# Weight copies of the second projection one tile at a time and earlier, early weights of the first feed-forward layer split ahead, three square sums added by transfers

## The chip, the cores and the metric

The kernel runs on one core of a Trainium2 chip. The metric is device time in microseconds (us). Three runs of the kernel before took 1983.63, 1984.63 and 1985.36 us, with a median of 1984.63. The execution that the profiler recorded took 1982.42 us, and its trace spans 1980.6 us from the first instruction to the last.

TensorE (PE) does the matmuls, VectorE (DVE), ScalarE (ACT) and GpSimd (POOL) the element work. Transfers are issued by SyncE (SP) and by POOL and are carried out by 16 DMA engines that the two queues share.

## The reference, cut to what matters

Two layers on a sequence of 1024 tokens of width 1024, in float32. Each layer is a token mixer and then a SwiGLU channel mixer, each with an RMSNorm ahead and a residual sum behind:

```python
def reference(x, conv_w_in, conv_w, conv_w_out, attn_w_qkv, ...):
    for i in range(DEPTH):                       # DEPTH = 2
        h = rmsnorm(x, norm_mixer[i])
        if i % N_MIXERS == 0:                    # layer 0
            mix = short_conv_mixer(h, conv_w_in[j], conv_w[j], conv_w_out[j])
        else:                                    # layer 1
            mix = swa_sink_attention(h, ...)
        x = x + mix
        h = rmsnorm(x, norm_ffn[i])
        x = x + swiglu_ffn(h, ffn_w_gate_up[i], ffn_w_down[i])

def short_conv_mixer(h, w_in, conv_w, w_out):
    b_gate, c_gate, xv = jnp.split(h @ w_in, 3, axis=-1)
    u = b_gate * xv
    y = <causal convolution of u, 3 taps for each channel>
    return (c_gate * y) @ w_out

def swiglu_ffn(h, w_gate_up, w_down):
    g, u = jnp.split(h @ w_gate_up, 2, axis=-1)
    return (jax.nn.silu(g) * u) @ w_down
```

The change lies in layer 0: the product with `w_out` (the second projection of the convolution mixer), the RMSNorm behind it, and the first product of the channel mixer (`w_gate_up`, called `w_gu` in the kernel).

## The kernel before, in words

**Layout.** Activations are kept transposed: features on the 128 partitions, 1024 tokens along the free dimension, so the eight tiles X0 to X7 hold the whole residual. A token half (512 columns) is called `h` = 0 or 1.

**Three matmuls for one.** Weights and activations are each split into a rounded part (`hi`, a CAST on ACT, L925) and the rest (`lo`, a subtraction on DVE, L926), in a type that the PE multiplies fast. Three matmuls (hi by hi, hi by lo, lo by hi; lines L992, L993, L995) replace one float32 product.

**Seven products for eight.** The large products are done as a fast 2-by-2 block multiplication: seven products, numbered `k` = 0 to 6, of sums and differences of the weight quarters and of the activation quarters. A *granule* is one such product for one pair of output tiles `u`: 4 weight tiles of 128 x 128, 12 matmuls of 128 x 512. Three of the seven take a weight quarter as it is; the other four take a sum of quarters.

**Where the sums of weights come from.** For most units DVE makes them. For the first four units of a product the four sums are made in DRAM ahead of time: `added_sums` (L883) has SP copy the four quarters into a scratch tensor (`s`), L886, and then POOL issue four transfers that add one quarter onto another, L889. It is called for `w_out` (L383, scratch `s_389`, in two pairs of tiles u = 0 and 2) and, through `first_added_sums` (L896), for `w_gu` (scratch `s_0_112`). Each copy moves two tile pairs at once: 512 KB, rows of 2 KB.

**What sets the order.** An object `Line` holds a planned clock in us, in which a matmul counts 0.2265. `at(t, f)` puts a piece of work at a planned time, `work` puts matmuls at the end of the line. The pieces are then written out in the order of planned time, and every engine, SP and POOL among them, works through its own list in that order. So whatever waits on an engine holds up all that stands behind it there. In this kernel planned time 0 is 41.48 us in the trace.

**The ring of weights.** `ring_granule` (L999) gives each granule a load (L969, 256 KB, into one of two buffers named WR or one of two named WH) planned 20 us ahead of its matmuls (`LEAD + 7`, LEAD = 13) and a split (L925, L926, into one of eight G buffers) planned 13 us ahead. Units from the fifth on load 512 KB at a time, into the same WR and WH buffers (L629, L633).

**The first mixer's middle and end.** After the first projection's start (to 52 us in the trace) come its granules, first k = 0, 1, 6, 5, 2, 3, 4 for four units, then unit by unit. Products that go to the PSUM banks P0 and P1 use them in turn, so a bank has to be read out before the next but one granule begins; the `acc` banks are four. `lead_in` (L727) then does the second projection: while the last unit of the first is finished, sums of activation quarters are made by transfers that add (L731, POOL); the granules of `w_out` follow, k = 0 first, each with four units. Results of some go to X by ACT (L776) and get the residual by a transfer that adds `xT` (L777, POOL); others are added by DVE (L781).

**The norm behind it.** `tail_done` (L1138) runs when a half tile is finished: ACT squares it (L1146 the first time, into the sum `s0` or `s1`; L1149 afterwards, into G10 or G11), POOL stores it (L1152), and DVE adds the square to the sum (L1154). `half_chain` (L1159) has PE sum over the partitions (L1167), once per half, turn the result into rows (L1179), and `scale` (L1189) multiplies. The half 1 sum is needed while PE works on the first granules of the channel mixer.

Of the kernel before, what the change touches and what calls it, by code (L numbers as in the profile page):

```python
# [13 lines left out]
ALU = mybir.AluOpType  # L14

P = 128
# [56 lines left out]
GROUP = 4  # L73
HALF = T // 2
# [5 lines left out]
LEAD = 13.0  # L80
# [3 lines left out]
def trunk_kernel(ctx: ExitStack, tc: tile.TileContext, xT, small, w_in, w_out, w_qk, w_v, w_o, w_gu, w_dn, out):  # L84
# [212 lines left out]
    def conv_layer():  # L297
# [81 lines left out]
        out_sums = tc.dram_tile((4, GROUP, P, 5 * P), F32, name="s3")  # L379
        for u in (0, 2):  # L380
            dst = [out_sums[i, u : u + 2][:, :, 0 : 4 * P] for i in range(4)]
            parts = [w_out[2 * u + r : 2 * u + 4 : 2][:, :, c] for r in (0, 1) for c in (0, 1)]
            added_sums(dst, parts, line, 60.0 + 9.0 * u, 18.0)  # L383
        first_added_sums(0, line, 120.0, 18.0)
        at(-7.6, mean)
        at(-5.0, turn)
        tools = scheme(line, ["G0", "G3", "G6", "G7", "G1", "G2", "G4", "G5"])
# [329 lines left out]
        def out_product(u, k):  # L717
            srcs = {0: w_out[2 * u][:, 0], 1: w_out[2 * u][:, 1], 4: w_out[2 * u + 1][:, 1]}
            src = srcs[k] if k in srcs else out_sums[SUMS[k], u][:, 0 : 4 * P]
            name = {1: "d1", 5: "e", 6: "e"}.get(k, "d")  # L720
            tag = "acc" if k in (0, 2, 3, 4) else f"P{u % 2}" if k == 1 or u < 2 else "acc"
            get = bank_at(("out", u), name, tag)
            ring_granule(4, lambda: Z[k], 0, get, k in (0, 1, 5), True, src=src)
            odd, h = C_OF[k]
            return get, 2 * u + odd, h

        def lead_in(done):  # L727
            s = line.end

            def add_by_dma(to, of):  # L730
                nc.gpsimd.dma_start(to(), of(), accum_op=ALU.add)  # L731

            def add_here(out_, a, b):
                dve.tensor_tensor(out_(), a(), b(), ALU.add)

            def x_of(m, h):
                return xT[m * P : (m + 1) * P, halves[h]]

            def load_half(m, h):
                nc.sync.dma_start(Y[m][:, halves[h]], x_of(m, h))  # L740

            for j in range(NK):
                at(s + 5.0, lambda j=j: X.__setitem__(j, Y[j]))
            for p in range(4):
                b11, b12, b21, b22 = (lambda j=2 * p + odd, h=h: Y[j][:, halves[h]] for odd in (0, 1) for h in (0, 1))
                t2 = lambda p=p: z2(p)
                k0, k1, k2, k3, k4, k5, k6 = (
                    (-7.6, 0.3, 7.0, 11.0, 27.4, 4.6, 36.0),
                    (-6.5, 1.0, 9.8, 12.4, 28.5, 5.7, 37.1),
                    (-5.4, 2.4, 15.0, 13.8, 29.6, 8.6, 38.2),  # L750
                    (1.7, 17.3, 24.9, 25.9, 30.7, 24.0, 39.3),
                )[p]
                if p < 3:
                    t_1, t_c, t_2, t_3, t_4 = ((-4.4, 0.2, 1.6, 3.6, 8.2), (-3.5, 1.2, 2.6, 4.5, 9.2), (-2.6, 7.6, 9.4, 5.4, 15.0))[p]
                    at(s + t_1, add_by_dma, b11, b12)
# [12 lines left out]
                put_z(2, p, t2, s + k2)  # L768
                put_z(3, p, b12, s + k3, minus=True)
                put_z(4, p, b21, s + k4, minus=True)  # L770
                put_z(6, p, b22, s + k6)
                at(s + k4 + 3.5, load_half, 2 * p + 1, 0)

            def copy_out(get, m, h, t, sign):
                c = halves[h]
                at(t, lambda: act.activation(X[m][:, c], get(), AF.Copy, scale=sign))  # L776
                at(t + 0.9, lambda: nc.gpsimd.dma_start(X[m][:, c], x_of(m, h), accum_op=ALU.add))  # L777

            def add_out(get, m, h, t, op):
                c = halves[h]  # L780
                at(t, lambda: dve.tensor_tensor(X[m][:, c], X[m][:, c], get(), op))  # L781

            v = n_units - 1
            first = {}
            for k in (2, 5, 3):
                steady(v, k)
            for u in (0, 1):
                first[u] = out_product(u, 0)
            steady(v, 4)
            first[2] = out_product(2, 0)  # L790
            steady(v, 6)
            first[3] = out_product(3, 0)
            for k in range(1, KINDS):
# [12 lines left out]
            return begin1, line.end  # L806

        channel_mixer(
            0,
            2,  # L810
            None,
            [],
            raw_tags=None,
            extra_tags=None,
            keep_tags=None,
            line=line,
            lead_in=lead_in,
# [65 lines left out]
    def added_sums(dst, parts, line, t, gap):  # L883

        def copy(i):
            nc.sync.dma_start(dst[i], parts[i])  # L886
# [48 lines left out]
    def scheme(line, ring_tags, before=None):  # L935
# [60 lines left out]

                line.work(3, three)

        def ring_granule(n, ops_of, j, bank_of, start, stop, src=None, raw_of=None, room=None, split=True, lo_eng=dve):  # L999

            it = {}
            t = line.end
            if src is not None:
                at(t - LEAD - 7.0, load_raw, it, src, n)
                raw_of = lambda: it["raw"]
            if split:
                split_granule(it, raw_of, n, room or ring_room, t - LEAD, lo_eng)
# [46 lines left out]
    def channel_mixer(layer, next_stage, src_of, operands, raw_tags, extra_tags, keep_tags, slots, begin_with=(), first_w=None, line=None, lead_in=None, before=None):  # L1054
# [83 lines left out]
        def tail_done(h, m, t):  # L1138
            c = slice(h * HALF, h * HALF + HALF)
            first = h not in begun  # L1140
            begun.add(h)

            def square():
                if first:
                    state["ss", h] = slot(f"s{h}", (P, HALF))
                    act.activation(state["ss", h], X[m][:, c], AF.Square)  # L1146
                else:
                    units["sq", h, m] = slot(f"G{10 + m % 2}", (P, HALF))
                    act.activation(units["sq", h, m], X[m][:, c], AF.Square)  # L1149

            at(t + 0.8, square)
            at(t + 0.9, lambda: nc.gpsimd.dma_start(xres[m][:, c], X[m][:, c]))  # L1152
            if not first:
                at(t + 1.6, lambda: dve.tensor_tensor(state["ss", h], state["ss", h], units["sq", h, m], ALU.add))  # L1154


# [33 lines left out]

        whole = layer == 0
        if whole:
            begin1, begin2 = lead_in(tail_done)
        else:
            origin = line.end
            begin1 = origin + 8 * tail
            begin2 = origin + 16 * tail
            for h in (0, 1):
                for m in range(NK):
                    tail_item(h, m)  # L1200
# [18 lines left out]
                nc.sync.dma_start(pairs[0]["s2"][:, u], first_sums[layer][SUMS[2], u][:, 0 : 4 * P])  # L1219


        if not whole:
# [69 lines left out]
        def unit_product(u, k, tag, direct):  # L1292
# [3 lines left out]
            ops_of = lambda: B[k]  # L1296
            if u < GROUP:
                srcs = {0: w_gu[layer, u][:, 0], 1: w_gu[layer, u][:, 1], 4: w_gu[layer, NF + u][:, 1]}
                if k < 3 and not whole:
                    it = early[k, u]  # L1300
                    granule_work(it, 4, ops_of, 0, get, start, True)
                    if k < 2:
# [929 lines left out]
```

## Time and profile before

| | us |
|---|---|
| runs, median of 3 | 1984.63 |
| profiled execution, its own time | 1982.42 |
| its span | 1980.6 |
| PE busy in the span | 1929.6 |
| DVE busy in the span | 1285.6 |
| ACT busy in the span | 876.7 |
| POOL busy in the span | 272.9 |

How to read it: PE has work nearly all the time, so what matters are the places where it had none, and what it waited for there. A group line gives engine, line, operation, the tile written, the tiles read, busy time and mean duration. A wait line gives who waited, on what engine and line, the sum in us, how often, and the longest. A line of a window gives, for a stretch of time, the busy us of each engine with the number of instructions, then the TensorE clock that was granted (1.00 is full), the mean busy share of the 16 DMA engines, and the GB/s moved. Numbers such as L886 are lines of the kernel before; in the changed kernel the same code lies 4 to 17 lines further down.

### The profile page before, as it was taken

The page shows a single profiled execution, that of the slowest core. Times are in us where ns is not written, and L with a number is a line of the kernel's source. Part 1 is how long each engine was busy: PE and PEld are TensorE (multiplying, and loading weights), DVE is VectorE, ACT ScalarE, POOL GpSimd, SP SyncE. Part 2 cuts the span into 40 slices and gives each one's busy share as a digit, 9 for nine tenths or more (in the row PEclk, how much of TensorE's full clock was granted, in tenths as well). Part 3 has the DMA queues.
Part 4 walks back from the last instruction along what each step waited for, and adds up shares of the span by engine and source line. Part 5 has one row for each costly group of instructions (what it writes and reads, how often), then busy time and mean ns, then how long its engine had stood idle before and what let it go on. Part 6 is the DMA issues. An engine that isn't in the chain of part 4 may idle for free.

```text
span 1980.6 us, 25183 instructions
## 1 busy us (share of the span) xinstructions
PE 1929.6 (97%) x9105; PEld 1612.1 (81%) x9105; DVE 1285.6 (65%) x2222; ACT 876.7 (44%) x1741; POOL 272.9 (14%) x370
## 2 busy tenths in 40 slices
PE   9976998999999999999999999999999999999999
PEld 8854887788888888888888888888888888888887
DVE  8964875876665656556644777788666566575543
ACT  5522354453333334344523888755333333344442
POOL 0000023101111110010012446410010111110000
PEclk9997999999999999999999999999999999999999
DMA  8433889455665663996420000051565665467562
GB/s 317 161 108 104 241 171 220 145 181 164 207 190 152 189 171 137 360 290 208 162 75 12 22 17 17 27 181 59 207 190 170 193 182 172 130 235 272 202 223 104
DMA packets 131404, 325.35 MB, mean 164 GB/s; under 512 B 13392, under 2 KB 24784, under 8 KB 131280
## 3 DMA queue, kind: packets, MB, share of 16 engines
q1 hardware_dynamic: 101280, 228.81, 33.2%
q0 software_dynamic: 29856, 94.91, 19.5%
q8 instruction: 71, 1.16, 0.2%
q14 instruction: 53, 0.43, 0.1%
q10 hardware_dynamic: 144, 0.03, 0.0%
HBM read 261.31 MB, written 130.55 MB: 198 GB/s over the span
## 4 chain that ended last, share of the span: by engine, by line
PE 85%; DVE 5%; DMA 5%; issue 3%; ACT 1%; POOL 1%; POOLq 0%; ACTq 0%; DVEq 0%
PE acc L992 14%; PE acc L993 14%; PE acc L995 14%; PE P L992 8%; PE P L993 8%; PE P L995 8%; PE acc L167 6%; DMA WR<-in_w_in 4%; PE acc L171 3%; PE P L1857 1%; DVE G L926 1%; PE P L1681 1%; PE P L1882 1%; PE acc L1122 1%; PE acc L1124 1%
## 5 line engine op out<-in xcount | busy, mean ns | idle before, releaser
L992 PE MATMUL acc<-XS,G 128*128 128x512 f32 x942 | 368.5, 391 | 18.9 <-ACT G L555 18.9
L993 PE MATMUL acc<-XS,G 128*128 128x512 f32 x942 | 367.6, 390 | 0.0
L995 PE MATMUL acc<-XS,G 128*128 128x512 f32 x942 | 367.4, 390 | 0.0
L992 PE MATMUL P<-A,G 128*128 128x512 f32 x534 | 209.7, 393 | 21.2 <-DVE G L543 14.1
L992 PEld LDWEIGHTS acc<-XS,G 128*128 128x128 f32 x942 | 177.6, 189 | 56.2 <-ACT G L555 19.3
L993 PE MATMUL P<-A,G 128*128 128x512 f32 x534 | 208.8, 391 | 0.0
L995 PE MATMUL P<-A,G 128*128 128x512 f32 x534 | 208.7, 391 | 0.0
L995 PEld LDWEIGHTS acc<-XS,G 128*128 128x128 f32 x942 | 177.6, 189 | 37.2
L993 PEld LDWEIGHTS acc<-XS,G 128*128 128x128 f32 x942 | 177.7, 189 | 36.7
L926 DVE TENSOR_TENSOR G<-WR,G 128x512 fp32r<-128x512 f32 (+1 forms) x218 | 145.8, 669 | 70.0 <-ACT G L925 69.4
L925 ACT CAST G<-WR 128x512 fp32r<-128x512 f32 (+1 forms) x218 | 131.8, 605 | 111.5 <-DMA WR<-in_w_in 49.4
L992 PE MATMUL acc<-A,G 128*128 128x512 f32 x458 | 178.3, 389 | 0.0
L995 PE MATMUL acc<-A,G 128*128 128x512 f32 x458 | 178.2, 389 | 0.0
L993 PE MATMUL acc<-A,G 128*128 128x512 f32 x458 | 178.2, 389 | 0.0
L926 DVE TENSOR_TENSOR G<-WL,G 128x512 fp32r<-128x512 f32 x168 | 114.9, 685 | 69.5 <-ACT G L925 69.5
L167 PE MATMUL acc<-XS,WH 128*128 128x512 f32 x480 | 148.0, 408 | 0.5 <-ACT WH L139 0.4
L925 ACT CAST G<-WH 128x512 fp32r<-128x512 f32 (+1 forms) x176 | 105.9, 602 | 87.4 <-PE acc L995 43.2
L992 PEld LDWEIGHTS P<-A,G 128*128 128x128 f32 x534 | 101.0, 189 | 43.5 <-DVE G L543 15.0
L926 DVE TENSOR_TENSOR G<-WH,G 128x512 fp32r<-128x512 f32 (+1 forms) x176 | 116.9, 664 | 20.2 <-ACT G L925 20.1
L1290 ACT ACTIVATE G<-G 128x512 f32<-128x512 f32 x88 | 55.8, 634 | 160.4 <-DVE G L1361 156.3
L925 ACT CAST G<-WL 128x512 fp32r<-128x512 f32 x168 | 103.4, 615 | 37.8 <-DVE WL L878 21.3
L995 PEld LDWEIGHTS P<-A,G 128*128 128x128 f32 x534 | 100.9, 189 | 21.2
(317 smaller groups left out, 3616.2 us busy)
## 6 DMA issues: line engine op xcount, KB each, us to landing
G<-h SPq DMA_DIRECT2D x70, 512.0 KB, 3.8
s<-in_w_dn SPq DMA_DIRECT2D x32, 704.0 KB, 7.9
h<-X POOLq DMA_DIRECT2D x44, 512.0 KB, 5.5
s<-s POOLq DMA_DIRECT2D x32, 704.0 KB, 7.4
WR<-in_w_gu SPq DMA_DIRECT2D x36, 512.0 KB, 4.8
WH<-in_w_gu SPq DMA_DIRECT2D x36, 512.0 KB, 3.8
h<-X POOLq DMA_DIRECT2D x66, 256.0 KB, 2.9
WR<-s SPq DMA_DIRECT2D x62, 256.0 KB, 4.6
```

Source lines behind the costliest of these rows:

```text
L167: pe.matmul(ps.half(h), wh, xs[:, j, c], start=first and j == 0, stop=False)
L171: pe.matmul(ps.half(h), wl, xs[:, 0, c], start=False, stop=last)
L925: lambda: act.copy(out_hi, raw),
L926: lambda: lo_eng.tensor_tensor(out_lo, raw, plain(out_hi), ALU.subtract),
L992: pe.matmul(ps, w[:, 0, c], x[:, 0, :], start=start and e == 0, stop=False, skip_group_check=True)
L993: pe.matmul(ps, w[:, 0, c], x[:, 1, :], start=False, stop=False, skip_group_check=True)
L995: pe.matmul(ps, w[:, 1, c], x[:, 0, :], start=False, stop=last, skip_group_check=True)
L1122: pe.matmul(ps, hi[:, kc], xs[:, 0, c], start=k == 0, stop=False, skip_group_check=True)
L1124: pe.matmul(ps, lo[:, kc], xs[:, 0, c], start=False, stop=k == n_op - 1, skip_group_check=True)
L1290: state["silu"] = act.activation(x, x, AF.Silu)
L1681: pe.transpose(pb[:, t], wide[:, t], ident)
L1857: pe.transpose(ps[:, kb, e, :], s[:, e, kb * P : (kb + 1) * P], ident)
```

## The change

Five edits, all in layer 0:

1. The copies of `w_out` quarters are issued one tile pair at a time (16 copies of 256 KB, 128 rows each, where 8 copies of 512 KB took two tile pairs whose places in `w_out` are not adjacent), and planned from 30.0 on in steps of 4.5 us, the two groups 4 us apart; before from 60.0 on in steps of 9 us, the groups 18 us apart. The adding transfers follow at 9 us where they were 18 us apart.
2. The copies of `w_gu` quarters keep their shape (8 of 512 KB) and are planned from 74.0 on with half the spacing; before from 120.0.
3. The weights of the first four granules (k = 0) of the channel mixer are loaded into XS0 in four transfers and split into XS6 and XS7, planned 34.7 us behind the start `s` of `lead_in` and then every 2.72 us; before they went through the ring like the others.
4. The second projection's last granules (k = 6) are loaded and split 6 us earlier (`lead=19.0`).
5. For half 1, the squares of tiles 3, 5 and 7 are added to `s1` by transfers that POOL issues, not by DVE. The two buffers of the squares are used in turn (`m // 2`), where before all odd tiles shared one and all even tiles the other.

```diff
-            parts = [w_out[2 * u + r : 2 * u + 4 : 2][:, :, c] for r in (0, 1) for c in (0, 1)]
-            added_sums(dst, parts, line, 60.0 + 9.0 * u, 18.0)
-        first_added_sums(0, line, 120.0, 18.0)
+            parts = [[w_out[2 * (u + i) + r][:, c] for i in (0, 1)] for r in (0, 1) for c in (0, 1)]
+            added_sums(dst, parts, line, 30.0 + 2.0 * u, 9.0)
+        first_added_sums(0, line, 74.0, 9.0)
...
-            ring_granule(4, lambda: Z[k], 0, get, k in (0, 1, 5), True, src=src)
+            ring_granule(4, lambda: Z[k], 0, get, k in (0, 1, 5), True, src=src, lead=19.0 if k == 6 else LEAD)
...
-            return begin1, line.end
+            return begin1, line.end, s + 34.7
...
-            raw_tags=None,
-            extra_tags=None,
+            raw_tags=("XS0",),
+            extra_tags=("XS6", "XS7"),
...
         def copy(i):
-            nc.sync.dma_start(dst[i], parts[i])
+            if isinstance(parts[i], list):
+                for j, part in enumerate(parts[i]):
+                    nc.sync.dma_start(dst[i][j], part)
+            else:
+                nc.sync.dma_start(dst[i], parts[i])
...
+            turn_ = m // 2 if layer == 0 else m
...
-                    units["sq", h, m] = slot(f"G{10 + m % 2}", (P, HALF))
+                    units["sq", h, m] = slot(f"G{10 + turn_ % 2}", (P, HALF))
...
-            if not first:
+            if not first and layer == 0 and h == 1 and m % 2:
+                at(t + 1.6, lambda: nc.gpsimd.dma_start(state["ss", h], units["sq", h, m], accum_op=ALU.add))
+            elif not first:
                 at(t + 1.6, lambda: dve.tensor_tensor(state["ss", h], state["ss", h], units["sq", h, m], ALU.add))
...
+        if whole:
+            def load_k0():
+                pairs[0]["k0"] = slot(raw_tags[0], (P, GROUP, 4 * P))
+                for u in range(GROUP):
+                    nc.sync.dma_start(pairs[0]["k0"][:, u], w_gu[layer, u][:, 0])
+            at(early_time - 9.0, load_k0)
+            for u in range(GROUP):
+                split_granule(early[0, u], lambda u=u: pairs[0]["k0"][:, u], 4, extra_rooms[u], early_time + 2.72 * u)
```

What this does to the lists of the engines, at three places. The first is SP's list where the `w_out` copies stand. Before, with WR and WH the loads of weights (256 KB at L969, 512 KB at L629 and L633):

```order
L969 DMA WR_1051<-in_w_in 128x512
L969 DMA WH_1073<-in_w_in 128x512
L629 DMA WR_1089<-in_w_in 128x1024
L633 DMA WH_1096<-in_w_in 128x1024
L886 DMA s_389<-in_w_out 256x1x512 x3
L629 DMA WR_1189<-in_w_in 128x1024
L633 DMA WH_1238<-in_w_in 128x1024
L886 DMA s_389<-in_w_out 256x1x512 x3
L629 DMA WR_1340<-in_w_in 128x1024
```

And now, where `s_0_391` and the like are sums stored earlier by the kernel itself:

```order
L973 DMA WR_772<-s_2_392 128x512
L888 DMA s_389<-in_w_out 128x512 x2
L973 DMA WH_796<-s_3_393 128x512
L888 DMA s_389<-in_w_out 128x512 x2
L973 DMA WR_820<-s_0_390 128x512
L888 DMA s_389<-in_w_out 128x512 x2
L973 DMA WH_844<-s_1_391 128x512
L888 DMA s_389<-in_w_out 128x512 x4
L973 DMA WR_873<-s_2_392 128x512
L973 DMA WH_898<-s_3_393 128x512
L888 DMA s_389<-in_w_out 128x512 x4
L973 DMA WR_925<-s_0_390 128x512
```

The copies have left the place among the 512 KB loads; the first of them stands eleven loads earlier, among 256 KB loads. Between those 512 KB loads now stand copies of `w_gu`.

The second place is POOL's list around the second projection. Before, with `s_0_112` the sums of `w_gu`, X and WL the activation sums, `in_xT` the residual:

```order
L731 DMA WL_2108<-X_220_1404 128x512
L889 DMA s_0_112<-s_0_112 256x512 x2
L731 DMA X_237_1542<-WL_2108 128x512
L777 DMA X_253_1653<-in_xT 128x512
L777 DMA X_197_1218<-in_xT 128x512
```

And now:

```order
L893 DMA s_389<-s_389 256x512 x8
L893 DMA s_0_112<-s_0_112 256x512 x8
L731 DMA X_253_1678<-X_253_1678 128x512
L731 DMA X_197_1241<-X_197_1241 128x512
L731 DMA X_220_1430<-X_220_1430 128x512
```

All sixteen additions of weight sums now stand ahead of the first activation sum; before, five of them stood among L731 and L777.

The third is DVE's list ahead of the half 1 sum. Before, with `s_385` that sum and G_403 to G_411 squares; L781 adds a product to X, L1189 scales, L926 splits:

```order
L1154 TENSOR_TENSOR s_385_2650<-s_385_2650,G_403_2747 128x512
L1189 SCALAR_TENSOR_TENSOR X_275_1845<-X_275_1845,cst_61,P_392_2682 128x512
L781 TENSOR_TENSOR X_253_1653<-X_253_1653,P_379_2617 128x512
L926 TENSOR_TENSOR XS_396_2701<-X_275_1845,XS_396_2701 128x512
L926 TENSOR_TENSOR G_405_2767<-WR_2704,G_405_2767 128x512
L1189 SCALAR_TENSOR_TENSOR X_195_1195<-X_195_1195,cst_61,P_392_2682 128x512
L1154 TENSOR_TENSOR s_385_2650<-s_385_2650,G_406_2772 128x512
L781 TENSOR_TENSOR X_197_1218<-X_197_1218,P_383_2640 128x512
L926 TENSOR_TENSOR XS_408_2787<-X_195_1195,XS_408_2787 128x512
```

And now, where the row of L1161 is the first addition to the sum (`s_388`) that DVE does:

```order
L1196 SCALAR_TENSOR_TENSOR X_275_1863<-X_275_1863,cst_61,P_394_2704 128x512
L781 TENSOR_TENSOR X_253_1678<-X_253_1678,P_384_2646 128x512
L930 TENSOR_TENSOR XS_397_2720<-X_275_1863,XS_397_2720 128x512
L1196 SCALAR_TENSOR_TENSOR X_195_1216<-X_195_1216,cst_61,P_394_2704 128x512
L1161 TENSOR_TENSOR s_388_2675<-s_388_2675,G_402_2779 128x512
L781 TENSOR_TENSOR X_197_1241<-X_197_1241,P_387_2667 128x512
L930 TENSOR_TENSOR XS_404_2793<-X_195_1216,XS_404_2793 128x512
```

Three of the seven additions and the splits of the first weights (G_405 is one of them) are gone from this stretch; four additions remain, all behind the three transfers that add.

More of the change, by code (lines that the diff above doesn't have):

```diff
@@ L997, in granule_work, with ring_granule @@
                 line.work(3, three)
-        def ring_granule(n, ops_of, j, bank_of, start, stop, src=None, raw_of=None, room=None, split=True, lo_eng=dve):
+        def ring_granule(n, ops_of, j, bank_of, start, stop, src=None, raw_of=None, room=None, split=True, lo_eng=dve, lead=LEAD):
             it = {}
@@ L1003, in ring_granule @@
             if src is not None:
-                at(t - LEAD - 7.0, load_raw, it, src, n)
+                at(t - lead - 7.0, load_raw, it, src, n)
                 raw_of = lambda: it["raw"]
             if split:
-                split_granule(it, raw_of, n, room or ring_room, t - LEAD, lo_eng)
+                split_granule(it, raw_of, n, room or ring_room, t - lead, lo_eng)
             granule_work(it, n, ops_of, j, bank_of, start, stop)
@@ L1192, in channel_mixer @@
         if whole:
-            begin1, begin2 = lead_in(tail_done)
+            begin1, begin2, early_time = lead_in(tail_done)
         else:
@@ L1219, in load_s2 @@
                 nc.sync.dma_start(pairs[0]["s2"][:, u], first_sums[layer][SUMS[2], u][:, 0 : 4 * P])
-        if not whole:
+        if whole:
[6 more added lines that the diff above has]
+                split_granule(early[0, u], lambda u=u: pairs[0]["k0"][:, u], 4, extra_rooms[u], early_time + 2.72 * u)
+        else:
             for u in range(GROUP):
@@ L1298, in unit_product @@
                 srcs = {0: w_gu[layer, u][:, 0], 1: w_gu[layer, u][:, 1], 4: w_gu[layer, NF + u][:, 1]}
-                if k < 3 and not whole:
+                if k < 3 and not whole or k == 0:
                     it = early[k, u]
                     granule_work(it, 4, ops_of, 0, get, start, True)
-                    if k < 2:
+                    if k < 2 and not whole:
                         at(line.end, lambda: ring.append(it["tag"]))
```

## The prediction, written before the changed kernel ran

> **What bounds the kernel now.** I read the page first, then PE's waits over the whole span, then, for each wait, the chain of work that ended last and the lists of the engines that it runs through.
>
> The page's first block, and the list of PE's waits (who waits for whom, us in total, times, longest):
>
> ```profile
> PE 1929.6 (97%) x9105; PEld 1612.1 (81%) x9105; DVE 1285.6 (65%) x2222; ACT 876.7 (44%) x1741; POOL 272.9 (14%) x370
> ...
> PE acc L992 <- ACT G L555: 18.9, 1, 18.9
> PE P L992 <- DVE G L543: 14.1, 1, 14.1
> PE P L992 <- DVE X L781: 7.0, 1, 7.0
> PE P L1167 <- DVE s L1154: 3.5, 1, 3.5
> ...
> PE P L992 <- DVE G L1328: 1.2, 2, 0.8
> ```
>
> PE is the bound, with 51.0 us idle in 1980.6. These five rows hold 44.7 of them, and all lie in layer 0 between 130 and 390 us. The first two, 33.0 us, are in the first mixer. The engine named there is only the last link; what the link waits for stands in the chain and in SP's list (start, duration):
>
> ```profile
> 129.12 22.42 DMA WR<-in_w_in
> 164.69 41.37 DMA WR<-in_w_in x2
> ...
> 109.87 19.13 SPq L886 DMA_DIRECT2D s<-in_w_out  x3
> 129.12 10.02 SPq L629 DMA_DIRECT2D WR<-in_w_in  x1
> 141.11 23.47 SPq L886 DMA_DIRECT2D s<-in_w_out  x3
> 164.69 11.23 SPq L629 DMA_DIRECT2D WR<-in_w_in  x1
> ```
>
> Three copies of `w_out` hold SP for 19 us, the next three for 23 us, and the 512 KB weight loads L629 stand behind them. How fast such copies run is seen in the windows (busy us of PE, PEld, DVE, ACT, POOL, then clock, DMA share, GB/s):
>
> ```profile
> 70.00:95.00 25.00, 24.93 (x110) 20.30 (x110) 22.99 (x38) 13.68 (x25) 0.00 (x0) 1.00 0.34 98
> 125.00:200.00 75.00, 42.05 (x171) 33.89 (x171) 33.46 (x52) 16.18 (x29) 3.68 (x4) 0.80 0.39 112
> 150.00:165.00 15.00, 11.62 (x44) 9.49 (x45) 12.44 (x20) 6.20 (x11) 0.92 (x1) 0.78 0.14 52
> 200.00:225.00 25.00, 25.00 (x112) 20.71 (x111) 19.59 (x31) 10.87 (x19) 1.88 (x3) 1.00 0.84 236
> 250.00:255.00 5.00, 5.00 (x24) 4.14 (x23) 4.05 (x7) 1.73 (x3) 0.90 (x1) 1.00 0.40 70
> 436.00:450.00 14.00, 14.00 (x64) 11.58 (x63) 10.46 (x18) 3.63 (x7) 0.54 (x1) 1.00 0.83 301
> ```
>
> From 150 to 165 us almost only `w_out` copies run: 52 GB/s at a share of 0.14, about two of 16 engines. From 436 to 450 the same kind of copy, of `w_dn` with 128 rows, runs at 301 GB/s at 0.83, so 363 GB/s at full share. The copy with two tiles outermost is confined; its bytes (8 x 512 KB, 4.19 MB) need 81 us at 52 GB/s.
>
> **The change part by part.** *The `w_out` copies.* With one tile pair each, all 128 rows outermost, they have the form of the `w_dn` copies, so I price them at 363 GB/s: 11.6 us of full share. They now stand between planned 30.0 and 47.5, 71.5 to 89 us in the trace, among the 256 KB loads, whose share there is 0.34: 17.5 x 0.34 = 6.0 us. Together 17.6 us of work in 17.5 us. Behind a waiting copy on SP stand those loads; DVE and ACT wait for them in their order, and PE for DVE. The room is large, since a load is planned 7 us ahead of its split and lands in about 2.6 us:
>
> ```profile
> DMA to landing us min/median/max: 2.4/2.6/11.1
> ```
>
> Bounds: 0 if copies run like the `w_dn` ones. If they run like POOL's additions in the window from 250 (70 GB/s at 0.40, 175 at full share), they take 24 us, the backlog grows to 12.5 us, a load lands 2.6 + 12.5 - 7 = 8.1 us late for its split, and with 2.7 us before the P banks are needed again PE stops for 5.4 us. I take 0.5, near the first, whose rows are copies too.
>
> *The stalls that go.* With the copies gone from among L629, 18.9 + 14.1 = 33.0 us. Each stall also leaves a slow clock:
>
> ```profile
> 153.38 0.80 PE acc L992
> 154.17 0.43 PE acc L993
> 157.44 0.23 PE acc L993
> ```
>
> The first seven matmuls behind the stall take 0.43 and more where 0.23 is usual: 0.57 + 6 x 0.20, about 1.7 us; the same behind each stall. So 36.4 us leave here. The cover that must hold instead is DVE: in the stretch from 125 to 200 it works 33.5 us, and without the 36.4 us it has 38.6 us for them (87%). From 200 to 225 it runs at 78% and from 70 to 95 at 92% with no wait of PE, so I charge nothing; below nothing can't be, above nothing is a rival.
>
> *The `w_gu` copies* keep their form and come to planned 74.0 to 96.5, 115 to 138 us. In the window from 200 to 225, where some of them run now at a share of 0.84, PE doesn't wait. Their loads are those of L629, planned 25 to 32 us ahead of the matmuls. Cost 0; if that cover failed it would be the old kind of stall, counted in the first rival. The *additions by POOL* of both groups come to 94 to 125 and 138 to 174 us. Two of them and one load fill 0.40 x 5 + 0.65 x 5 = 5.3 us of full share between 250 and 260:
>
> ```profile
> 255.00:260.00 5.00, 5.00 (x24) 4.14 (x23) 1.29 (x2) 2.56 (x5) 0.89 (x1) 1.00 0.65 127
> ```
>
> Less 0.7 for the load, 2.3 us each; eight in 31 us are a share of 0.6 beside loads of 0.34. Full, not over.
>
> *The 7.0 us.* POOL's part of the chain; how long the addition of weight sums issued at 289.74 took to land, then the residual transfers L777 issued from 299 to 301 and at 305; and the matmul that waited:
>
> ```profile
> 291.54 7.43 issue
> 298.98 3.74 DMA X<-in_xT
> 302.81 0.70 DVE X L781
> ...
> DMA to landing us min/median/max: 8.9/8.9/8.9
> ...
> DMA to landing us min/median/max: 3.7/5.4/5.6
> DMA to landing us min/median/max: 7.6/7.6/7.6
> ...
> 303.55 0.79 PE L992 MATMUL P<-A,G 128*128 128x512 f32 x1 [7.02 <-DVE X L781]
> ```
>
> 289.74 + 8.9 = 298.6: POOL issues its next transfer when the addition of weight sums has landed. The order now has all sixteen of these ahead of L731, which begins at 262 us before. The residual transfer was planned 21.1 us behind `lead_in`'s start (262.1 + 4.4 = 266.5), so at 287.6. It lands 3.7 to 7.6 us later, as those rows do, and DVE is done by 296.0 at worst; PE had to stop at 296.5. So the 7.0 us go, and with them 1.7 us of slow clock: 8.7. Bounds: 8.7, and 5 if the four loads into XS0 (1 MB, 2.9 us at full share), planned 25.7 us behind `lead_in`'s start, delay that transfer's followers.
>
> *The half 1 sum.* Six splits and three additions, 9 x 0.6 = 5.4 us, leave DVE ahead of the sum, but the first addition DVE still does now waits for a chain of three transfers, each waiting for the one before.
>
> ```profile
> 351.00 0.75 DVE L1189 SCALAR_TENSOR_TENSOR X<-X,cst,P 128x512 f32<-128x512 f32 x1
> 359.70 0.68 DVE L1154 TENSOR_TENSOR s<-s,G 128x512 f32<-128x512 f32 x1
> 373.39 0.68 DVE L1154 TENSOR_TENSOR s<-s,G 128x512 f32<-128x512 f32 x1
> 374.22 1.03 PE L1167 MATMUL P<-cst,s 128*128 128x1 f32 x8 [3.48 <-DVE s L1154]
> ...
> L731 POOL DMA_DIRECT2D X<-X x2: 885/1014/1143, 262.1 to 262.7; - x2
> DMA to landing us min/median/max: 3.2/3.7/4.1
> ...
> DMA to landing us min/median/max: 5.5/6.4/6.9
> ```
>
> The last row is of L777's transfers from 341 to 343. In the trace's time of before (only shifted later): DVE comes to its first addition eleven instructions behind the scaling at 351.0, held up by the matmuls that end at 358.3, so at about 360.3. The first transfer can go at 351.6, when its square is done. The nearest rows are L731's, additions from SBUF to SBUF: 3.2 to 4.1 us, median 3.7. Three with 0.1 us between: 362.9. Then the addition and 15 instructions at 0.62 (13.69 us for 22 between 359.70 and 373.39): 372.8 where it was 374.1. So PE waits 2.2 us where it waited 3.5, a gain of 1.3; the slow clock and the 1.2 us of the fifth row stay. Bounds: at 3.2 us DVE waits 1.1 us and PE 0.8; at 6.4 us, the median of that last row, the third lands at 371.0 and PE waits 10.4 us, a loss of 6.9.
>
> [...] No addition in these rows is under 3.2, so I stay with the rows.
>
> *Splits moved ahead* (k = 0 in XS6 and XS7, k = 6 six us sooner): six splits on DVE and ACT of 0.7 us each go to 301 to 310 and 326 to 334 us of before's time, where DVE has room:
>
> ```profile
> 325.00:350.00 25.00, 25.00 (x116) 20.82 (x115) 12.42 (x23) 10.51 (x21) 10.73 (x14) 1.00 1.03 240
> ```
>
> Four loads replace four. Cost 0; with no room, each split would delay by its 0.7 us what stands behind it.
>
> Sum: 33.0 + 3.4 + 8.7 + 1.3 - 0.5 = 45.9. Against the profiled execution's 1982.4 us this is 1936.5. The median of the runs is 2.2 us above that execution, so the forecast is 1939.
>
> **The rivals.** *A: the burst costs time by the piece.* If each copy occupied the queue for the 2.6 us in which a 256 KB load lands, 16 of them are 41.6 us, with the loads 47.6 in 17.5: loads up to 30 us late, less 7.1 of room, about 20 us of stall: 1959. [...] Against it: loads that land in 2.6 us overlap in the 301 GB/s of the window from 436, made of transfers of 704 KB and less. The milder form is the bound above, or DVE at 87% no longer catching up, 5 to 12 us: 1944 to 1951. *B: the chain of transfers is slow*, as L777's rows are: 8 us more than forecast, 1947. Against: the share there was 0.53 in all, and loads have left it. *C: slower than before.* A copy of one tile is confined to fewer engines still. Copies at rate R end 4.19 MB / R behind 71.5 us, and the load that stands behind the fourteenth is due at PE at 107 (the 21st granule, 2.72 us each from 52.4): from about 52 GB/s down the stall eats the whole gain, and on one engine, half of today's, 161 us leave about 126 us of stall: 2064. Against: all 128-row rows above. *D: the change doesn't do what it says*: the copies stay at 52 GB/s, so 81 us leave 46 us of stall, only sooner: 1984.
>
> **How the numbers follow.** Forecast (1933 to 1944) 0.62; A 0.05 for the strong form and 0.15 for the mild; B 0.13; C 0.02; D 0.03. The likeliest is 1939. The range goes from 1932, where nearly all of the 51.0 idle us are gone, to 1956, which takes in B and the milder A. A measurement of this kernel can tell 0.2% (4 us) from no change. Forecast, A and B are faster by more: 0.95; D is the same or nearly: 0.03; slower 0.02.
>
> **What would show it.** In the changed kernel's profile: SP issues each `w_out` copy in under 1 us; the DMA share from 70 to 90 us is near 1.0 at over 280 GB/s; no wait of PE for L555 or L543; POOL's additions of weight sums end before L731 begins, and no wait for L781's line over 1 us; the wait of PE ahead of L1167's line, 0.8 to 4 us, ends behind DVE's additions, and the first of these has waited for a DMA. I am wrong if PE waits between 75 and 200 us by more than 5 us in all (A), or if the third adding transfer lands over 4.5 us after its issue (B).

## The result, and the profile after

Three runs of the changed kernel took 1937.32, 1938.33 and 1939.72 us. The ratio of its time to the time before is 0.9768, with a 95% interval of 0.9746 to 0.9790. The profiled execution is the one of 1938.33 us, with a span of 1936.6 us: 44.0 us under the span before.

The page's first block and the list of PE's waits of the changed kernel (who waits for whom, us in total, times, longest). L1174 was L1167 before, L1161 was L1154, L996 was L992, L1345 was L1328; further on, L1196 was L1189, L929 and L930 were L925 and L926, L893 was L889 and L973 was L969. In the kernels of the experiments the numbers shift by a few lines more.

```profile
PE 1924.2 (99%) x9105; PEld 1609.3 (83%) x9105; DVE 1283.4 (66%) x2219; ACT 877.6 (45%) x1741; POOL 275.7 (14%) x373
...
PE P L1174 <- DVE s L1161: 2.5, 1, 2.5
...
PE P L996 <- DVE X L781: 1.2, 1, 1.2
PE P L996 <- DVE G L1345: 1.2, 2, 0.8
```

The 51.0 idle us of PE are 12.4 now, and PE is busy 5.4 us less with the same 9105 matmuls, which is the slow clock that followed the stalls (0.80 granted from 125 to 200 us before, 1.00 now). The rows for L555 and L543 (33.0 us) are gone, L781 went from 7.0 to 1.2, the sum's wait from 3.5 to 2.5.

SP's list in the stretch of the burst (start, duration), with L888 for the copies of `w_out`, which was L886:

```profile
70.41 1.22 SPq L888 DMA_DIRECT2D s<-in_w_out  x2
72.10 0.33 SPq L973 DMA_DIRECT2D WH<-s  x1
72.48 1.13 SPq L888 DMA_DIRECT2D s<-in_w_out  x2
...
87.67 1.65 SPq L888 DMA_DIRECT2D s<-in_w_out  x2
```

A pair of copies holds SP for about 1.2 us, where three held it for 19 to 23 us, and all 16 are issued between 70.4 and 89.3 us. The loads L973 stand between them and are issued at once. What the engines did meanwhile, in the windows (busy us of PE, PEld, DVE, ACT, POOL, then clock, DMA share, GB/s):

```profile
70.00:95.00 25.00, 24.93 (x110) 20.31 (x109) 22.98 (x38) 13.15 (x24) 0.98 (x1) 1.00 0.87 253
...
90.00:95.00 5.00, 5.00 (x24) 4.14 (x23) 4.92 (x9) 2.83 (x5) 0.00 (x0) 1.00 1.04 260
125.00:200.00 75.00, 75.00 (x332) 62.10 (x331) 65.29 (x102) 28.40 (x50) 9.85 (x11) 1.00 0.79 194
```

From 70 to 95 us the DMA share rose from 0.34 to 0.87, and PE works exactly as long as before (24.93). From 125 to 200 PE works 75.00 of 75 us where it worked 42.05.

POOL's list around the place of the 7.0 us (start, duration, in brackets the idle time ahead and what ended it):

```profile
198.37 0.90 POOL L893 DMA_DIRECT2D s<-s  x1 [5.24 <-DVE WL L871]
225.09 2.70 POOL L731 DMA_DIRECT2D X<-X  x3 [25.82 <-ACT G L929]
...
252.60 1.90 POOL L777 DMA_DIRECT2D X<-in_xT  x2 [2.77 <-ACT X L776]
257.84 0.87 POOL L777 DMA_DIRECT2D X<-in_xT  x1 [3.34 <-ACT X L776]
```

The last of the sixteen additions of weight sums (L893) is issued at 198.37, so POOL is free when L731 begins at 225.09, and the residual transfer L777 waits only for its data. Before, POOL stood 7.43 us behind an addition there.

The end of half 1, first POOL's three adding transfers (L1159), then DVE:

```profile
307.62 0.89 POOL L1159 DMA_DIRECT2D s<-G  x1
...
311.79 0.88 POOL L1159 DMA_DIRECT2D s<-G  x1 [1.06 <-ACT XS L929]
...
315.67 0.89 POOL L1159 DMA_DIRECT2D s<-G  x1 [1.65 <-ACT XS L929]
```

```profile
315.80 0.74 DVE L1196 SCALAR_TENSOR_TENSOR X<-X,cst,P 128x512 f32<-128x512 f32 x1
319.04 0.69 DVE L1161 TENSOR_TENSOR s<-s,G 128x512 f32<-128x512 f32 x1 [2.50 <-DMA s<-G]
...
328.42 0.68 DVE L1161 TENSOR_TENSOR s<-s,G 128x512 f32<-128x512 f32 x1
```

DVE comes to its first addition at 316.54 and stands 2.50 us until the third transfer has landed. That is the length of PE's wait at the sum, 9 us later.

### The profile page after: what moved, and what is told of

Same layout as the page of the kernel before. It is cut to its first block, busy times and chain, and to the rows that moved or that the text cites. A ratio compares the mean times of both kernels' runs of the same rounds, so it can differ in the third digit from the quotient of the medians.

```text
span 1936.6 us, 25190 instructions
## 1 busy us (share of the span) xinstructions
PE 1924.2 (99%) x9105; PEld 1609.3 (83%) x9105; DVE 1283.4 (66%) x2219; ACT 877.6 (45%) x1741; POOL 275.7 (14%) x373
## 4 chain that ended last, share of the span: by engine, by line
PE 91%; DVE 3%; issue 3%; DMA 1%; ACT 1%; POOL 1%; POOLq 0%; DVEq 0%; ACTq 0%
PE acc L996 15%; PE acc L999 15%; PE acc L997 15%; PE P L996 9%; PE P L997 9%; PE P L999 9%; PE acc L167 7%; PE acc L171 3%; PE P L1874 1%; PE P L1698 1%; PE P L1899 1%; PE acc L1126 1%; PE acc L1128 1%; PE acc L1127 1%; PE P L1900 1%
## 5 line engine op out<-in xcount | busy, mean ns | idle before, releaser
L996 PE MATMUL acc<-XS,G 128*128 128x512 f32 x926 | 360.4, 389 | 0.0
L999 PE MATMUL acc<-XS,G 128*128 128x512 f32 x926 | 360.3, 389 | 0.0
L997 PE MATMUL acc<-XS,G 128*128 128x512 f32 x926 | 360.2, 389 | 0.0
L996 PE MATMUL P<-A,G 128*128 128x512 f32 x534 | 208.0, 390 | 1.3 <-DVE X L781 1.2
L999 PEld LDWEIGHTS acc<-XS,G 128*128 128x128 f32 x926 | 173.8, 188 | 36.2
L996 PEld LDWEIGHTS acc<-XS,G 128*128 128x128 f32 x926 | 173.8, 188 | 36.0
L997 PEld LDWEIGHTS acc<-XS,G 128*128 128x128 f32 x926 | 173.9, 188 | 35.9
L996 PE MATMUL acc<-A,G 128*128 128x512 f32 x458 | 178.3, 389 | 0.0
L929 ACT CAST G<-WR 128x512 fp32r<-128x512 f32 (+1 forms) x216 | 130.6, 605 | 73.0 <-PE acc L999 31.7
L930 DVE TENSOR_TENSOR G<-WR,G 128x512 fp32r<-128x512 f32 (+1 forms) x216 | 144.3, 668 | 27.7 <-ACT G L929 26.8
L930 DVE TENSOR_TENSOR G<-WL,G 128x512 fp32r<-128x512 f32 x168 | 114.9, 685 | 70.0 <-ACT G L929 70.0
L929 ACT CAST G<-WH 128x512 fp32r<-128x512 f32 (+1 forms) x174 | 104.7, 602 | 88.9 <-PE acc L999 39.6
L930 DVE TENSOR_TENSOR G<-WH,G 128x512 fp32r<-128x512 f32 (+1 forms) x174 | 115.5, 664 | 16.6 <-ACT G L929 16.5
L996 PEld LDWEIGHTS P<-A,G 128*128 128x128 f32 x534 | 100.3, 188 | 22.7 <-DVE X L781 1.6
L929 ACT CAST G<-WL 128x512 fp32r<-128x512 f32 x168 | 103.4, 615 | 34.0 <-DVE WL L878 21.2
```

Of the source, the lines that this page charges most:

```text
L929: lambda: act.copy(out_hi, raw),
L930: lambda: lo_eng.tensor_tensor(out_lo, raw, plain(out_hi), ALU.subtract),
L996: pe.matmul(ps, w[:, 0, c], x[:, 0, :], start=start and e == 0, stop=False, skip_group_check=True)
L997: pe.matmul(ps, w[:, 0, c], x[:, 1, :], start=False, stop=False, skip_group_check=True)
L999: pe.matmul(ps, w[:, 1, c], x[:, 0, :], start=False, stop=last, skip_group_check=True)
```

## The experiments

The theory: the copy with two tiles outermost is confined (to about two of the 16 DMA engines, an estimate from its share of 0.14) and holds SP (19 and 23 us for three copies), so its form makes the two large stalls; POOL's order makes the 7.0 us; splits moved ahead and adding transfers relieve DVE at the sum. The main rivals were that planning the copies sooner is what matters, that the size of the copies or that the two tiles are not adjacent is what matters, and that the parts at the sum bring nothing or cost.

**Form alone, at the old times.** The kernel before, with only this:

```diff
-            parts = [w_out[2 * u + r : 2 * u + 4 : 2][:, :, c] for r in (0, 1) for c in (0, 1)]
+            parts = [[w_out[2 * (u + i) + r][:, c] for i in (0, 1)] for r in (0, 1) for c in (0, 1)]
```

> The kernel before with one edit: the w_out copies one tile pair at a time (16 of 256 KB), at the planned times of before. If the form of the copy (two tiles outermost, two DMA engines) made both first stalls, they go: 33.0 us and 3.4 us of slow clock, so about 1948 us; the wait for L781 (7.0 us) and the one ahead of the half 1 sum (3.5 us) stay. If the place of the copies in SP's list made them (they came too late), the stalls stay and the time is about 1984.

Measured: 1945.45 us, ratio to before 0.9802 (0.9786 to 0.9818). Its two largest waits:

```profile
PE P L996 <- DVE X L781: 6.8, 1, 6.8
PE P L1171 <- DVE s L1158: 3.5, 1, 3.5
```

The 33.0 us are gone, the other two waits stand as before. So the form is worth some 39 of the 46 us, without any copy being planned sooner.

**Sooner alone, in the old form.** The changed kernel with the line above turned back, so 8 copies of 512 KB from 30.0 on:

> The changed kernel with one edit undone: the w_out copies move two tile pairs each again, at the new, earlier times. If the form is the cause, 4.19 MB at 52 GB/s take 81 us from 70 us on, and the loads among them come some 46 us late: a new stall of that size between 95 and 160 us, about 1986 us in all. If coming sooner was what helped, the time stays near 1939.

Measured: 2004.47 us (two runs), ratio 1.0101 (1.0081 to 1.0121), slower than before. PE's largest waits, SP's list and the windows:

```profile
PE acc L996 <- ACT XS L929: 25.1, 1, 25.1
PE P L996 <- DVE G L543: 23.1, 2, 16.2
PE P L996 <- ACT G L593: 8.2, 2, 7.8
```

```profile
85.81 0.63 SPq L890 DMA_DIRECT2D s<-in_w_out  x1
86.54 9.96 SPq L973 DMA_DIRECT2D WH<-s  x1
96.55 10.72 SPq L890 DMA_DIRECT2D s<-in_w_out  x2
107.37 8.50 SPq L973 DMA_DIRECT2D WR<-s  x1
```

```profile
90.00:95.00 5.00, 0.00 (x0) 0.00 (x0) 0.00 (x0) 0.08 (x1) 0.00 (x0) 0.90 0.13 51
90.00:157.00 67.00, 26.60 (x84) 20.23 (x84) 11.13 (x19) 8.11 (x15) 2.77 (x3) 0.68 0.29 78
```

The rate is the one expected, 51 GB/s at a share of 0.13. A load of 256 KB now takes about 10 us to be issued (9.96 in the row above, 12.50 at most). That is about what one copy of 512 KB needs at 51 GB/s (10.3 us), so SP seems to go on only when a copy ahead of the load has ended. The direction was expected, the size was not: PE's waits in the first mixer come to 56.8 us (the three rows and 0.4 for L555), not 46, and PE is busy 1935.0 us, 10.8 more than in the changed kernel. Together 67.6, and the span is 67.2 longer. My sum had neither the slow clock (0.68 on average here) nor the time in which DVE catches up with the splits.

**Rows outermost, two tiles inside.** The changed kernel with 8 copies of 512 KB, whose outermost dimension is the 128 rows:

```diff
+            elif dst[i].tensor.name.startswith("s3"):
+                nc.sync.dma_start(dst[i].rearrange("u p c -> p u c"), parts[i].rearrange("u p c -> p u c"))
```

> The changed kernel, but with 8 copies of 512 KB that take the same two tile pairs with the 128 rows outermost and the two tiles inside. If the outermost count of 2 confines a copy, this one is not confined: 1938 us, and a DMA share near 0.87 from 70 to 95 us. If a copy over two tiles that are not adjacent, or the size of 512 KB, is slow by itself, the stall of the two-tile form is back: about 1985.

Measured: 1939.14 us, ratio 0.9773 (0.9758 to 0.9787), like the changed kernel. From 70 to 95 us:

```profile
70.00:95.00 25.00, 24.93 (x111) 20.29 (x110) 22.98 (x38) 13.24 (x25) 1.29 (x2) 1.00 0.89 271
```

Same size and same non-adjacent tiles as in the slow kernel, only the order of the dimensions differs. So neither the size nor the adjacency made the stalls, and "one tile at a time" isn't what helps: the rows being outermost is.

**Four tiles outermost.** The changed kernel with four copies of 1 MB, `w_out[i // 2 : i // 2 + 7 : 2]`, four tiles outermost:

> The changed kernel, but with 4 copies of 1 MB that take four tile pairs each, the four outermost. If the outermost count sets the number of DMA engines, these run on four, at about 104 GB/s (a share of 0.25 of their own), 40 us in all where the two-tile form takes 81: copies end near 113 us, the load behind the last one is due at 105, so a stall of 8 to 10 us and a time of about 1947. If every form but 128 rows outermost is equally slow: 1985. If size is what helps: 1938.

Measured: 1964.69 us, ratio 0.9900 (0.9886 to 0.9915). In a window in which SP was held at one load (86.92 to 96.88 us) and POOL issued nothing:

```profile
90.00:95.00 5.00, 1.25 (x6) 0.71 (x4) 0.00 (x0) 0.00 (x0) 0.00 (x0) 0.87 0.26 103
```

103 GB/s at 0.26, where the two-tile copy had 51 at 0.13: twice. So in these three forms share and rate go by the count of the outermost dimension: 0.13 and 51 GB/s for two, 0.26 and 103 for four, and for 128 rows, with the loads beside them from 70 to 95 us, 0.87 and 253 or 0.89 and 271. That two tiles outermost mean about two of the 16 engines and four about four is an estimate from these shares. The size was missed again in the same way: waits of 18.2 us in the first mixer, and PE busy 9.6 us more.

**The two-tile copies from ACT's queue.** As in the second experiment, but issued by ACT, while the loads stay on SP:

```diff
+            elif dst[i].tensor.name.startswith("s3"):
+                nc.scalar.dma_start(dst[i], parts[i])
```

> The changed kernel with the w_out copies in the two-tile form, as early as in the second experiment, but issued from ACT's queue, while the loads stay on SP's. Theory that a copy confined to two engines holds the queue that issues it: ACT is held for about 10 us by each copy as SP was, so its splits stop and with them PE, 45 us or more of stall, time 1985 to 2010. Rival, that only loads behind the copies in the same queue suffer: ACT issues each copy in about 1 us, the copies run to 152 us beside the loads, no stall over 3 us between 70 and 160, and only POOL's additions come later (up to 9 us at L781's place), time 1938 to 1948.

Measured: 1998.53 us, ratio 1.0071 (1.0051 to 1.0091). ACT's list, then SP's:

```profile
89.12 10.57 ACTq L890 DMA_DIRECT2D s<-in_w_out  x1
...
112.53 18.95 ACTq L890 DMA_DIRECT2D s<-in_w_out  x2
131.53 0.58 ACT L593 COPY G<-P 128x512 f32<-128x512 f32 x1 [18.38 <-issue]
```

```profile
78.37 0.32 SPq L975 DMA_DIRECT2D WH<-s  x1
91.35 0.32 SPq L975 DMA_DIRECT2D WR<-s  x1
```

SP issues its loads in 0.32 us again, but ACT is held for about 10 us by a copy and its read-outs and splits stand behind. So the confined copy held either engine that issued it. A slow queue beside the loads' queue was no way out here (1998.53 us), where the engine that feeds it has other work; an engine without any was not tried.

**The `w_gu` copies and additions at their old times.** The changed kernel with `first_added_sums(0, line, 120.0, 18.0)`:

> The changed kernel, with the copies and additions of the w_gu blocks back at their old planned times (from 120.0 in steps of 18.0). Theory that the 7.0 us wait for L781 was POOL's order, the residual transfers behind the additions of weight sums: the wait is 5 to 7 us again, with 1 to 2 us of slow clock, time 1944 to 1946, while no wait comes back in the first mixer. Rival, that other loads at that place made it: wait under 2 us, time 1938 to 1939.

Measured: 1951.86 us, ratio 0.9841 (0.9827 to 0.9854). Waits, and POOL's list:

```profile
PE P L996 <- DVE X L781: 9.5, 1, 9.5
PE P L1174 <- DVE s L1161: 5.6, 1, 5.6
```

```profile
254.94 0.89 POOL L893 DMA_DIRECT2D s<-s  x1 [7.60 <-issue]
255.51 1.22 POOL L731 DMA_DIRECT2D X<-WL  x1
264.12 2.68 POOL L777 DMA_DIRECT2D X<-in_xT  x3 [7.38 <-issue]
```

The wait for L781 is back, with POOL standing 7.38 us behind an addition of weight sums ahead of L777, and no wait came back in the first mixer. The mechanism holds. It costs 13.5 us, not 6 to 8: the wait is 2.5 us longer than before the change, and the sum's wait grew by 3.1: one of the three adding transfers took 5.1 us to land there, POOL stood 4.1 us for it, and DVE 5.31 us for the third, where it stood 2.50 in the changed kernel. PE is also busy 4.0 us longer (1928.2), which goes with the slow clock behind the two waits (0.76 from 265 to 285 us and 0.66 from 335 to 350, both 1.00 in the changed kernel). Why the wait for L781 is 9.5 and not 7.0 I did not settle.

**The parts at the sum, one at a time.** Four kernels with all copies as changed. *Transfers taken out* (the condition at L1158 replaced by `if False:`):

> The changed kernel, with the three square additions of half 1 back on DVE (no adding transfers). In the changed kernel DVE stands 2.5 us for the third transfer; three additions cost it 3 x 0.6 = 1.8 us. Theory that the transfers bring next to nothing: time 1938 (within 1.5 us of the changed kernel's 1938.3), PE's wait ahead of the sum 1.5 to 2.5 us. Rival, that the transfers carry the gain at the sum: the wait goes back to 3.5 us or more and the time is 1940 or over.

Measured: 1934.23 us, ratio to before 0.9754 (0.9741 to 0.9767). That is under both theories, and 4 us under the changed kernel. *Splits moved ahead taken out* (k = 0 through the ring, k = 6 with its usual lead):

> The changed kernel without the splits that were moved ahead (k = 0 goes through the ring again, k = 6 at its usual lead). Theory that they took 6 x 0.65 = 4 us of DVE work from ahead of half 1's sum: the third transfer now lands before DVE comes to it, so the 2.5 us of DVE's wait are filled first, and PE's wait ahead of the sum is 2.5 + (4 - 2.5) = 4 us, time 1939.5 to 1941 with slow clock. Rival, that DVE had room there anyway: wait 2.5 us, time 1938. Third, that all 4 us add: wait 6.5 us, time 1942.5 or over.

Measured: 1943.02 us, ratio 0.9795 (0.9782 to 0.9809). The third expectation held. *Both taken out*:

> The changed kernel without the splits moved ahead and without the adding transfers (only the copies and additions of weights are changed). Theory that at half 1's sum the splits moved ahead are what helps and the transfers cost: PE's wait ahead of the sum is 3.5 us as before the change (6.9 with the transfers alone, 0.6 with the splits alone, 2.5 with both), time 1937 to 1939, under the 1943 of the transfers alone. Rival, that the two parts need each other: wait 5 us or more, time 1941 or over.

Measured: 1938.80 us, ratio 0.9763 (0.9749 to 0.9776). PE's wait ahead of the sum, and the time:

| | three additions on DVE | three by transfer |
|---|---|---|
| splits as before | 3.5 us, 1938.8 | 6.9 us, 1943.0 |
| splits moved ahead | 0.6 us, 1934.2 | 2.5 us, 1938.3 |

In each row the transfers cost (3.4 and 1.9 us of wait), in each column the splits help (2.9 and 4.4). The times of the table come from different chips, on which the kernel before had medians between 1983.6 and 1986.0 us; so the waits, and not the times alone, carry the comparison. Where the 0.6 comes from is seen in DVE's list of the kernel without transfers:

```profile
306.27 0.75 DVE L1196 SCALAR_TENSOR_TENSOR X<-X,cst,P 128x512 f32<-128x512 f32 x1 [0.45 <-PE P L1186]
306.93 0.68 DVE L1161 TENSOR_TENSOR s<-s,G 128x512 f32<-128x512 f32 x1
307.70 0.69 DVE L930 TENSOR_TENSOR XS<-X,XS 128x512 fp32r<-128x512 f32 x1
...
315.75 0.74 DVE L1196 SCALAR_TENSOR_TENSOR X<-X,cst,P 128x512 f32<-128x512 f32 x1
316.41 0.68 DVE L1161 TENSOR_TENSOR s<-s,G 128x512 f32<-128x512 f32 x1
```

From the first scaling L1196 to the one ahead of the wait DVE takes 9.48 us here (306.27 to 315.75) with three additions in between, and 8.81 in the changed kernel (306.99 to 315.80) without them. The three cost it 0.67 us, not 1.8: without them DVE stands in this stretch twice for 0.69 us until ACT is done, and the additions fill these gaps. The transfers take away 0.67 us and add a wait of 2.50, a loss of 1.8; PE's wait differs by 1.9.

The clock behind PE's wait differs too. From 330 to 340 us, first the changed kernel, then the one without transfers, each with the sum's matmuls (L1174) and the fourth large matmul behind L1186, which turns the sum into rows:

```profile
330.00:340.00 10.00, 10.00 (x42) 8.14 (x41) 6.86 (x15) 3.96 (x9) 0.00 (x0) 0.83 0.23 70
329.24 1.02 PE L1174 MATMUL P<-cst,s 128*128 128x1 f32 x8 [2.52 <-DVE s L1161]
...
335.00 0.40 PE L996 MATMUL acc<-XS,XS 128*128 128x512 f32 x1
```

```profile
330.00:340.00 10.00, 10.00 (x47) 8.28 (x46) 9.60 (x15) 5.45 (x9) 0.00 (x0) 1.00 0.37 94
326.60 1.02 PE L1174 MATMUL P<-cst,s 128*128 128x1 f32 x8 [0.60 <-DVE s L1161]
...
330.81 0.40 PE L996 MATMUL acc<-XS,XS 128*128 128x512 f32 x1
```

Behind the wait of 2.5 us the granted clock is 0.83, behind the one of 0.6 it is 1.00. For the same matmuls between the two rows PE takes 5.76 us in the changed kernel (329.24 to 335.00) and 4.21 without the transfers (326.60 to 330.81). These 1.6 us agree with PE's busy time, 1924.2 and 1922.5 us in all, and come on top of the 1.9 us of wait.

With the splits as before, the transfers also hold ACT: its square at 318.99 stands 2.29 us until a transfer has read the buffer that it writes, one of two.

```profile
318.99 0.63 ACT L1154 ACTIVATE G<-X 128x512 f32<-128x512 f32 x1 [2.29 <-DMA s<-G]
```

**Two transfers of three.** Tiles 3 and 5 by transfer, tile 7 by DVE (`m in (3, 5)`):

> The changed kernel, with only the first two of the three additions by transfer, the third by DVE. The second transfer landed at 315.1 us, before DVE came there at 316.5, so DVE should wait for none and do one more addition (0.6). Theory that the chain's third link is what DVE waits for: PE's wait ahead of the sum 2.5 -> 0.6 to 1.0 us, time 1936.5. Rival, that DVE is held elsewhere: wait 2 us or more, time 1938.

Measured: 1937.06 us, ratio 0.9764 (0.9751 to 0.9778), PE's wait 2.5 us. DVE's row:

```profile
314.15 0.69 DVE L1161 TENSOR_TENSOR s<-s,G 128x512 f32<-128x512 f32 x1 [1.86 <-DMA s<-G]
```

The expectation left out that DVE's own addition of tile 7 comes where the third transfer was, at 312.3, ahead of the place where it had waited before. It waits 1.86 us there for the second transfer and does 0.6 more of work: 2.5 again. The time doesn't tell this kernel from the changed one.

**The better kernel, once more, beside the changed one.** Both on one chip:

> The changed kernel with the three square additions on DVE, once more, beside the changed kernel on one chip. Theory: 3 to 5 us under it (0.15 to 0.25%), PE's wait ahead of the sum 0.6 us. Rival, that the first comparison was scatter: within 2 us of it.

> The changed kernel itself, for the direct comparison. Theory: 1938 to 1939, PE's wait ahead of the sum 2 to 3 us. Rival, scatter: 1934 to 1936.

Measured: without the transfers 1934.71 us (1933.68 to 1936.22, four runs), ratio to before 0.9742 (0.9729 to 0.9755), PE's wait at the sum 0.6; the changed kernel 1938.47 us (1937.18 to 1940.06, five runs), ratio 0.9759 (0.9745 to 0.9772), wait 3.0. The means differ by 3.7 us, with a 95% interval of 1.8 to 5.6 worked out from these nine runs, so the kernel without transfers takes 0.9981 of the changed kernel's time (0.9971 to 0.9991). It is the best of the study.

The steps in a row, each from the medians given, which come from different chips: before 1984.6; form of the copies 1945.4; all weight copies and additions sooner 1938.8; splits ahead 1934.2 to 1934.7; the three transfers, back up to 1938.3 to 1938.5.

## Why the prediction was right, and where it was not

- *The two stalls, 33.0 us*: right. The copies' form accounts for them, as said; planning them sooner does not.
- *Slow clock, 3.4 + 1.7 = 5.1 us*: PE's busy time fell by 5.4.
- *The 16 copies between the loads, 0.5 us*: measured nothing. The copies land in 3.4 to 9.5 us (median 5.2), the share from 70 to 90 us is 0.82 at 252 GB/s, less than the "near 1.0 at over 280" that I named, and PE's busy time from 70 to 95 us did not change. Rivals A and C had no part in it.
- *The 7.0 us*: the mechanism was right, the size was 5.8. The margin that I found was half a microsecond at the slowest landing; DVE waited 0.64 us for the residual transfer ahead of 260.0, and PE 1.2, more than the 1 us that I had named as the limit. In the repeat of the changed kernel PE waited 0.2 there.
- *The half 1 sum, 1.3 us*: measured 1.0 (3.5 to 2.5), and the chain of transfers came out as long as worked out: from the first transfer's issue to the third's landing 11.4 us where it was 11.3, DVE's wait 2.50 where it was 2.6. Within the chain two errors cancel, which is luck: the transfers landed in 3.2 to 3.5 us where 3.7 was taken, and some 0.7 us passed between a landing and the next issue where 0.1 was. But the step that failed is in the prediction's sentence "Six splits and three additions, 9 x 0.6 = 5.4 us, leave DVE ahead of the sum". It priced the additions at their duration, though about two thirds of that fills gaps in which DVE waits for ACT without them. The term hid a gain of 2.9 us from the splits and a loss of 1.9 from the transfers. The sum came out near, the account of what helps did not.
- *The total*: predicted for the profiled execution 1936.5, measured 1938.3: of the 1.8 us between them 1.2 are what is left at L781 and 0.3 the sum; less 0.5 for the copies' burst and 0.3 of slow clock in its favour, about 1 us lies in small waits that I did not follow. I then added 2.2 us, by which the median before lay above its profiled execution; after the change the two are equal. That the forecast of 1939 is so near is partly this.
- *Rival D's price* (the copies stay slow, only sooner: 1984) was wrong by 20 us: the second experiment is that rival, and took 2004. Of those 20 us about half is slow clock, which the price left out (0.68 granted from 90 to 157 us, PE busy 10.8 us more than in the changed kernel), and the waits came to 56.8 us where 46 were worked out; that DVE's catching up makes this second part is argued, not shown.

## What to carry to other kernels

Look at the outermost dimension of a transfer's two access patterns before its size or place: two tiles outermost ran at 51 GB/s, the same bytes with 128 rows outermost left no trace in the time (1939.14 us, where the changed kernel took 1938.33), and the slow form held SP and ACT alike when they issued it, about 10 us for a load behind it on SP and for a copy on ACT. When work is moved off an engine, price it by what the engine's list gains between two fixed points, not by the duration of the instructions, and test parts that point the same way apart: here two of them shared a term of 1.3 us, and one of the two was a loss of 4 us.

## What the runs showed that I had not expected

- Behind PE's wait of 2.5 us at the sum the granted clock falls (0.83 over 330 to 340 us), behind the wait of 1.2 us at L781 it does not (1.00 from 245 to 265 us). The two are not alike: behind the wait at the sum PE first runs eight matmuls of one column, so 3.4 us (326.73 to 330.13) pass without a matmul of 512 columns, in the kernel without transfers only 1.5. No run here tests whether the wait itself or the small matmuls behind it make the difference.
- Three chained additions of 256 KB from SBUF to SBUF landed 3.2 to 3.5 us after issue in the changed kernel. Without the splits moved ahead, where loads through the ring stand at that place, the first two landed after 5.2 and 5.0 us and the third after 3.3 us; that the loads made the first two longer is my estimate, not shown.
- Moving a confined transfer sooner made the kernel slower than leaving it (2004.5 against 1984.6 us), though its stalls were the same kind. Before, the eight copies were issued over 79 us (99.7 to 178.8), about as fast as they run (81 us in all at 52 GB/s), and now they are planned within 17.5; that this is what makes the difference is argued, not shown.
